# Experts in groups of one larger and two smaller, between pairs, and the first loads rearranged

## The chip, the cores and the metric

The kernel runs on one core of one Trainium2 chip. The time is that of one execution on the device in microseconds. Three runs of the kernel before took 752.1 to 754.06 us, with a median of 753.59 us.

## The reference

One transformer layer on 512 tokens of width 1024, all in fp32: an RMS norm, one input projection that feeds two kinds of attention, one output projection into the residual stream, and then a mixture of 32 SwiGLU experts, of which each token uses two:

```python
h = rms_norm(x, g_attn[l])
proj = h @ w_in[l]                                   # 1024 x 3072
o_da = diff_attention(...)                           # 4 heads, two softmax maps per head
o_sb = stick_breaking(...)                           # 8 heads
x = x + jnp.concatenate([o_da, o_sb], axis=-1) @ w_o[l]
h2 = rms_norm(x, g_ffn[l])
# hier_moe: top-1 of 4 expert groups, then top-2 of 8 experts inside it
y = (jax.nn.silu(xb @ w1[e]) * (xb @ w3[e])) @ w2[e] # 1024 -> 512 -> 1024, for each expert e
```

Each expert has three matrices of 1024x512 fp32, 2 MiB each. All 32 experts are read: 192 MiB, most of the 228.86 MB that the page counts.

## The kernel before, in words

**First part.** The residual input arrives as x transposed (`xT`, eight slices of 128 rows) and as x (`x_t`, four tiles). The input projection's weights come in chunks of 256 columns, each in four pieces of 256 KB (`load_w`). fp32 products are made of rounded parts: ScalarE writes the rounded "high" part (`x_high` for x, `high` in `split_pieces` for weights), VectorE the rest (`x_low`, `low`), and TensorE multiplies the parts (`rows_bundles`, `cols_bundles`). While the first data is on its way, `keep_clock` gives TensorE 20 products of ones. `square` on ScalarE sums the squares of each of the four x tiles, from which `token_scales` makes the norm's factors. `Weave` mixes steps of the projection with the attention tasks; each engine then runs its own instructions in the written order.

**Experts.** Tokens are gathered for a group of experts at a time, 128 rows in all. Each expert has a *place*. The first `FIXED` = 4 places belong to experts 0 to 3, whose weights can be fetched before the routing is known. The rest are sorted by the number of their tokens (`sort_experts`, `name_experts`), so the transfers of a later place need a register that SyncE loads (`values_load` of `who_i`). Places below `SMALL` = 20 have 64 rows (`SLOTS`), the 12 others 32. There are 13 groups: ten pairs of 64-row experts, and at positions 2, 7 and 12 (from 0) a group of four 32-row experts. `hidden` multiplies a group's tokens by w1 and w3 in 16 steps, `outputs` by w2 in 8. A step has one product for each expert of the group; their results lie in different rows of the same PSUM bank. Between the steps stand pieces of the next group's gathering (`quarter`, L1164) and of the last one's return to the tokens (`combine`, L1325 and L1326).

**Transfers.** Every weight part of an expert (half of w1, w3 or w2) is one transfer of 1 MiB by SyncE's queue, into the next tile of a ring (`ring_tile`, list `slots`). The ring goes once through 19 tiles. The two parts of tile `ma` then leave it (`ma` becomes the running sum), so later rounds have 17. A part that has no free tile waits on SyncE until the products that read the tile's last content are done. Group 0's last part goes to `yh` and `yl` (`load_last`). `load_parts(i)` issues group i's transfers: part by part, in each part expert by expert. At group `PAUSE` = 7 stands the `If` of `overflow`, for experts with more tokens than rows.

Of the kernel before, what the change touches and what calls it, by code (L numbers as in the profile page):

```python
# [30 lines left out]
FIXED = 4  # L31
# [63 lines left out]
def tile_block(ctx: ExitStack, tc: tile.TileContext, a: dict, out: bass.AP):  # L95
# [45 lines left out]
    oh_rel, vneg = r_tile[0:32, 0, 0:640], r_tile[0:4, 1, 0:640]  # L141
    lamv, lam_p = r_tile[:, 0, 640:896].rearrange("p (a b) -> p a b", a=4), r_tile[:, 0, 896:960]
    rb = r_tile[0:32, 1, 640:644]
# [44 lines left out]
    g_col = const.tile([P, KC], F32, name="g_col")  # L188
    nc.scalar.dma_start(g_col, a["g_attn"][0].rearrange("(p k) -> p k", k=KC))
# [8 lines left out]
    gqk = const.tile([P, 2], F32, name="gqk")  # L198
    gsub = const.tile([P, 1], F32, name="gsub")
    gsb = const.tile([P, 1], F32, name="gsb")  # L200
    col = lambda ap, n: bass.AP(tensor=ap.tensor, offset=ap.offset, ap=[[1, n], [1, 1]])
    for m in range(2):
        rows = slice(64 * m, 64 * m + 64)
        nc.sync.dma_start(gqk[rows, 0:1], col(a["qn_g"], 64))
        nc.sync.dma_start(gqk[rows, 1:2], col(a["kn_g"], 64))
# [46 lines left out]
    for n in range(KC // 2):  # L252
        x_high(2 * n)
        high[n]()
        x_low(2 * n)
        low[n]()
        x_high(2 * n + 1)
        x_low(2 * n + 1)

    bt = pool_q8.tile([P, 4, 512], F32, tag="bt", name="bt")  # L260
    vdram = dram.tile([4, 640], F32, name="vdram")
    def small_loads():
        nc.sync.dma_start(rb, a["rel_bias"])
        nc.sync.dma_start(oh_rel, a["rel_onehot"])
        for m in range(2):
            nc.sync.dma_start(gsb[64 * m:64 * m + 64], col(a["sb_out_g"], 64))
        nc.sync.dma_start(gsub, col(a["subln_g"], 128))
        for i, n in enumerate(("lam_q1", "lam_k1", "lam_q2", "lam_k2")):
            s = a[n]
            nc.sync.dma_start(lamv[:, i], bass.AP(tensor=s.tensor, offset=s.offset, ap=[[0, P], [1, 64]]))  # L270
# [103 lines left out]
    def h_rows(i):  # L374


        pbs = [bank("mm", (P, 2, 256)) for _ in range(2 if i == 0 else 0)]
        for k in range(0, KC // 2, 2):
            for t0, pb in zip((0, 2), pbs):
                yield from rows_bundles(h_high, h_low, split[i], t0, pb, range(k, k + 2), k == 0, False)  # L380
        for t0 in (0, 2):
            pb = pbs[t0 // 2] if pbs else bank("sc" if (i, t0) == (1, 0) else "mm", (P, 2, 256))
            yield from rows_bundles(h_high, h_low, split[i], t0, pb, range(KC // 2 if pbs else 0, KC), not pbs)
            yield t0, pb
# [261 lines left out]
    for i, (g, n, j) in enumerate(ORDER):  # L646
# [10 lines left out]
    groups = [(0, 2), (2, 2), (20, 4), (4, 2), (6, 2), (8, 2), (10, 2), (24, 4), (12, 2), (14, 2), (16, 2), (18, 2),  # L657
              (28, 4)]
# [3 lines left out]
    slots = [("q8", tag, 2) for tag in ("bt", "qs", "kl", "kh")] + [("xs", "e0", 1), ("xs", "e1", 1)]  # L662
    slots += [("q8", tag, 2) for tag in ("qs", "kl", "kh")] + [("n", "n0", 1), ("n", "n1", 1)]
    slots += [("mx", "ma", 1), ("mx", "ma", 1), ("mx", "mb", 2)]
    slots += [("w8", tag, 2) for tag in ("w_h", "w_l", "w_h", "w_l")]
    slots += [("mx", "mb", 2)]
    slots[0] = ("q8", "bt", 1)

    def ring_tile():

        pool, tag, bufs = slots[ring[0] % len(slots)]
        ring[0] += 1
        if tag == "ma":
            if ring[0] > len(slots):
                return ring_tile()
# [15 lines left out]
    def load_parts(i):  # L691
        last = i == NG - 1
        first, n_exp = groups[i]
        if first < FIXED:
            who = [first + e for e in range(n_exp)]
        else:
            who = [nc.values_load(place_id[0][0:1, first + e:first + e + 1], engines=[mybir.EngineType.SP],
                                  min_val=0, max_val=NE - 1) for e in range(n_exp)]
        t = {}
        for n, h in hidden_order(i) + [("w2", 0), ("w2", 1)]:  # L700
            src = {"w1": w1, "w3": w3, "w2": w2}[n]
# [3 lines left out]
            for c, m in zip(cuts, cuts[1:]):  # L705
                for e in range(n_exp):
                    if (i, n, h, e) == (0, "w2", 1, 1):
                        continue
                    if c == 0:
                        t[n, h, e] = ring_tile()  # L710
                    dst, part = t[n, h, e], expert(who[e], h)(src)
                    if first >= FIXED:
                        part = part.rearrange("o p f -> p (o f)")
                    nc.sync.dma_start(dst[:, c:m], part[:, c:m])
                    if m == 2048:
                        yield t
# [9 lines left out]
    loads, ahead = load_parts(0), load_parts(1)  # L726

# [29 lines left out]
    gfp = const.tile([P, 2, 4], F32, name="gfp")  # L757
# [7 lines left out]
    def router_loads():  # L765
        nc.sync.dma_start(gfp, a["g_ffn"])
        raw_r = pool_at.tile([P, KC, 64], F32, tag="qn", name="raw_r", bufs=2)
        parts = {"w_router_g": raw_r[:, 0:1, 0:32], "w_router_e": raw_r[:, 1:5]}
        for n, r in (("w_router_g", 4), ("w_router_e", 32)):
            parts[n] = parts[n].rearrange("p a b -> p (a b)").rearrange("p (h c) -> p h c", h=2)  # L770
            nc.sync.dma_start(parts[n], a[n].rearrange("p h r c -> p h (r c)"))
        for src, c0, n in ((a["b_router_g"], 0, 4), (a["b_router_e"], 4, 32)):
            nc.sync.dma_start(rbias[:, c0:c0 + n], bass.AP(tensor=src.tensor, offset=src.offset, ap=[[0, P], [1, n]]))
# [14 lines left out]
        def gains():  # L788
            for n, c0, w in (("w_router_g", 0, 4), ("w_router_e", 4, 32)):
                nc.vector.tensor_tensor(wr[:, :, c0:c0 + w], parts[n].rearrange("p h (r c) -> p (h r) c", r=4),  # L790
                                        gfp.rearrange("p h r -> p (h r)").unsqueeze(2).to_broadcast([P, KC, w]),
                                        op=ALU.mult)
# [121 lines left out]
    def match(oh, rk, ts_):  # L914
        n = ts_.stop - ts_.start
        m, w = oh.shape[2:]
# [3 lines left out]
    def gather_part(px, oh, h, ts_):  # L920

        for t in ts_:
            x2 = x_tile[0][:, t, h * 512:(h + 1) * 512].rearrange("p (r b) -> p r b", r=4)
            one = oh[:, t].rearrange("p e s -> p (e s)").bitcast(F32)
# [38 lines left out]
    for t in range(NT):  # L963
        square(t)
    token_scales()
    wv.fill(16)
# [23 lines left out]
    next(ahead)  # L990
# [21 lines left out]
    oh0 = pools["n"].tile([P, NT, 2, SLOTS], F32R, tag="oh", name="oh", bufs=1)  # L1012
    def half_match(n, t):
        for _ in range(n):
            yield
        place(t)
        match(oh0, rank[:, :, 0:2], slice(t, t + 2))
# [32 lines left out]
    for _ in range(7):  # L1050
# [73 lines left out]
    def one_hot(rk, second=False):  # L1124
        n = rk.shape[-1]
        shape = [P, NT, n, P // n]
        if second:
            oh = wk("oht", shape, F32R, bufs=2)
        else:
            oh = pools["n"].tile(shape, F32R, tag="oh", name="oh", bufs=1)  # L1130
        match(oh, rk, slice(0, NT))
        return oh

    def dispatch(oh, p, px=None):
# [3 lines left out]
        ohs = [oh[:, t].rearrange("p e s -> p (e s)") for t in range(NT)]  # L1138
        n_exp, w_exp = oh.shape[2:]
        rows = [slice(w_exp * e, w_exp * e + w_exp) for e in range(n_exp)]  # L1140
        d = {"px": px, "parts": rows}

        spare = not isinstance(p, int)
# [43 lines left out]
        def finish(tag="mm"):  # L1187
# [15 lines left out]
            m = 3 * n_exp  # L1203
            g4 = pools["n"].tile([P, NT, 12], F32, tag="g4" + own, name="g4", bufs=bufs)
            c = 0 if spare else 6 * p
            for u, pb in enumerate(pbs):
                nc.scalar.copy(oht[:, 2 * u:2 * u + 2], pb[:, :, 0])
                nc.vector.tensor_copy(g4[:, 2 * u:2 * u + 2, :m], pb[:, :, 1, c:c + m])
            for e, part in enumerate(rows):
                x = 6 * (e // 2) + 2 * (e % 2)  # L1210
# [118 lines left out]
    def overflow():  # L1329
# [12 lines left out]
        with tc.If(rounds > 0):  # L1342
            move(rank_s[:, :, SMALL:], SLOTS // 2)
            with tc.For_i(0, rounds, 1):
                move(rank_s, -SLOTS)
                with tc.For_i(0, NP, 1) as iv:
# [5 lines left out]
                    dd = dispatch(one_hot(rk), own)  # L1352
# [29 lines left out]
    def group_dispatch(i, oh=None, px=None):  # L1382
        first, n = groups[i]
        if oh is None:
            oh = one_hot((rank if first < FIXED else rank_s)[:, :, first:first + n], i == 1)
        return dispatch(oh, first // 2, px)
# [18 lines left out]
    for i in range(NG):  # L1405
# [3 lines left out]
        if not last:  # L1409
            rest = ahead if i == 0 else load_parts(i + 1)  # L1410
            for nxt in islice(rest, 1) if i == PAUSE else rest:
                pass
        during, after = [[] for _ in range(16)], [[] for _ in range(8)]
        if i == 0:
# [4 lines left out]
            during[1] = [name_experts]  # L1419
# [4 lines left out]
        else:  # L1424
            for n in range(8):
                at_ = (3 if n < 4 else 7) if last else 3 + n // 2 if i == PAUSE else 4 + n // 2 * 2
# [119 lines left out]
```

## Time and profile before

| | |
|---|---|
| median of 3 runs | 753.59 us |
| the profiled execution | 753.97 us, of which the span from first to last instruction is 752.3 us |
| TensorE busy | 726.8 us (97% of the span) |
| VectorE, ScalarE, GpSimd busy | 389.1, 302.2, 91.7 us |
| moved by DMA | 228.86 MB, mean 304 GB/s |
| granted TensorE clock | 0.992 of full speed |

A slice of the page's second part is 18.8 us. Its lines PE and DMA are read together: PE is at 9 tenths nearly throughout, and DMA reaches 9 from the middle on. A busy PE is not one at its best rate, since the records of pipelined products overlap and their ends are modelled; whether TensorE waits is read from the distance between starts.

### The profile page before, as it was taken

The numbers are of one execution on the slowest core, as the hardware profiler recorded it, in microseconds if no ns is written. First come the engines' busy times: TensorE is split into PE (matmuls) and PEld (weight loads), VectorE is DVE, ScalarE is ACT, GpSimd is POOL, SyncE is SP. The second block draws the span as 40 slices with busy tenths as digits, with TensorE's granted clock in tenths as the row PEclk, the third lists the DMA queues.
The fourth block names the chain that finished last, engine by engine and source line by source line (L and its number), as shares of the span: only waits on it lengthen the run. The fifth ranks groups of instructions, "written<-read, shape, count | busy, mean of one in ns | idle before, by whom it ended". The sixth has DMA issues, their size and how long they took to land. (4 is left out here: it accounts for less than half of the span.)

```text
span 752.3 us, 13147 instructions
## 1 busy us (share of the span) xinstructions
PE 726.8 (97%) x4812; PEld 454.7 (60%) x4812; DVE 389.1 (52%) x919; ACT 302.2 (40%) x708; POOL 91.7 (12%) x175
## 2 busy tenths in 40 slices
PE   9999999999999999999999999999779999999986
PEld 9899988887989984554435444453233444535324
DVE  4577778776665462254444554443433544444413
ACT  6665776876755340232232323221222232232100
POOL 0302100466665020000000000000000000000000
PEclk9999999999999999999999999999998999999999
DMA  8432121322573986649999999999999999999998
GB/s 314 134 127 86 54 84 57 113 58 64 166 313 112 368 362 253 240 194 381 418 419 421 421 420 422 421 421 421 416 421 419 423 419 421 422 419 420 418 409 298
DMA packets 46638, 228.86 MB, mean 304 GB/s; under 512 B 6724, under 2 KB 9412, under 8 KB 23656
## 3 DMA queue, kind: packets, MB, share of 16 engines
q1 hardware_dynamic: 46152, 227.83, 76.3%
q8 instruction: 40, 0.66, 0.3%
q14 instruction: 30, 0.25, 0.1%
q10 hardware_dynamic: 416, 0.14, 0.1%
HBM read 225.83 MB, written 2.11 MB: 303 GB/s over the span
## 5 line engine op out<-in xcount | busy, mean ns | idle before, releaser
L1156 ACT CAST part<-xs 128x256 fp32r<-128x256 f32 x176 | 63.1, 406 | 146.6 <-PE ps_mm L1164 60.1
L1157 DVE TENSOR_TENSOR part<-xs,part 128x256 fp32r<-128x256 f32 x176 | 66.6, 419 | 58.7 <-ACT part L1156 58.7
L1327 DVE TENSOR_TENSOR sums<-ps_o,sums 128x512 f32<-128x512 f32 x88 | 56.7, 686 | 71.0 <-PE ps_o L1326 71.0
L313 PE MATMUL ps_mm<-w_h,hTl 128*128 128x256 f32 x240 | 69.3, 289 | 0.1
L1222 PE MATMUL ps_mm<-qs,xt 128*64 128x512 f32 (+1 forms) x136 | 67.8, 610 | 0.0
L313 PE MATMUL ps_mm<-w_h,hTh 128*128 128x256 f32 x240 | 67.3, 281 | 0.0
L313 PE MATMUL ps_mm<-w_l,hTh 128*128 128x256 f32 x240 | 67.3, 280 | 0.0
L1222 PE MATMUL ps_mm<-mb,xt 128*64 128x512 f32 (+1 forms) x120 | 59.0, 610 | 4.1 <-PEq L1342 4.1
L1222 PE MATMUL ps_mm<-kl,xt 128*64 128x512 f32 (+1 forms) x120 | 59.3, 610 | 0.0
L1222 PE MATMUL ps_mm<-w_l,xt 128*64 128x512 f32 (+1 forms) x128 | 50.7, 602 | 0.0
L1222 PE MATMUL ps_mm<-kh,xt 128*64 128x512 f32 (+1 forms) x104 | 50.4, 600 | 0.0
L1222 PE MATMUL ps_mm<-w_h,xt 128*64 128x512 f32 (+1 forms) x120 | 46.8, 601 | 0.0
L313 PEld LDWEIGHTS ps_mm<-w_h,hTl 128*128 128x128 f32 x240 | 45.3, 189 | 0.6 <-DVE qn L438 0.3
L313 PEld LDWEIGHTS ps_mm<-w_l,hTh 128*128 128x128 f32 x240 | 45.3, 189 | 0.1
L313 PEld LDWEIGHTS ps_mm<-w_h,hTh 128*128 128x128 f32 x240 | 45.2, 188 | 0.0
L180 DVE TENSOR_TENSOR w_l<-w_raw,w_h 128x512 fp32r<-128x512 f32 x64 | 44.2, 707 | 1.0 <-ACT w_h L177 0.6
L1325 PE MATMUL ps_o<-yl,oht 128*128 128x512 f32 x96 | 43.2, 450 | 0.6 <-DVE sums L1327 0.6
L518 DVE TENSOR_TENSOR_SCAN p<-p,ones_f 128x513 f32<-128x513 f32 (+3 forms) x32 | 27.5, 858 | 30.5 <-POOL p L513 30.5
L1325 PEld LDWEIGHTS ps_o<-yl,oht 128*128 128x128 f32 x96 | 17.9, 187 | 41.8 <-issue 18.8
L1164 PEld LDWEIGHTS ps_mm<-part,oh 128*128 128x128 f32 x160 | 21.8, 191 | 33.3 <-DVE part L1157 20.3
L1251 DVE SCALAR_TENSOR_TENSOR sl<-ps_mm,rsl,sl 128x256 f32<-128x256 f32 x26 | 11.4, 479 | 58.6 <-PE ps_mm L1222 58.4
L1271 ACT ACTIVATE yh<-ps_sc,gsl 128x512 fp32r<-128x512 f32 (+2 forms) x29 | 18.5, 643 | 55.2 <-PE ps_sc L1278 55.2
(295 smaller groups left out, 1786.5 us busy)
## 6 DMA issues: line engine op xcount, KB each, us to landing
qs<-in_w SPq DMA_DIRECT2D x22, 1024.0 KB, 19.7
e<-in_w SPq DMA_DIRECT2D x22, 1024.0 KB, 19.8
kl<-in_w SPq DMA_DIRECT2D x21, 1024.0 KB, 19.7
kh<-in_w SPq DMA_DIRECT2D x21, 1024.0 KB, 19.7
n<-in_w SPq DMA_DIRECT2D x20, 1024.0 KB, 19.8
mb<-in_w SPq DMA_DIRECT2D x20, 1024.0 KB, 19.8
w_h<-in_w SPq DMA_DIRECT2D x20, 1024.0 KB, 19.8
w_l<-in_w SPq DMA_DIRECT2D x20, 1024.0 KB, 19.7
```

What stands on the lines that cost most here:

```text
L180: eng.tensor_tensor(part(wl, n), raw[i, n], part(wh, n).bitcast(F32), op=ALU.subtract)
L313: nc.tensor.matmul(pb[:, u], lhsT=x(t0 + u, k), rhs=y[:, k], start=first, stop=last, skip_group_check=True)
L518: nc.vector.tensor_tensor_scan(rev, rev, ones_f[:, 0:1].to_broadcast([P, n + 1]), 1.0, op0=ALU.mult, op1=ALU.mult)
L1156: nc.scalar.copy(hi, whole)
L1157: nc.vector.tensor_tensor(lo, whole, hi.bitcast(F32), op=ALU.subtract)
L1164: nc.tensor.matmul(d["rows"][:, q * 256:q * 256 + 256], lhsT=ohs[t], rhs=d[n][:, m], start=(n % 8 == 0 and m == 1), stop=(n % 8 == 7 and m ...
L1222: nc.tensor.matmul(ph[n][part], lhsT=d["xt"][h][:, r, part], rhs=w, start=(h == 0 and r == 0), stop=(h == 1 and r == 3))
L1251: nc.vector.scalar_tensor_tensor(s, ph["w3"][:, c], d["rsl"], s, op0=ALU.mult, op1=ALU.mult)
L1271: nc.scalar.activation(yh, py, AF.Copy, scale=gsl)
L1325: nc.tensor.matmul(pc, lhsT=oht[:, t], rhs=yl[:, c], start=True, stop=False)
L1327: nc.vector.tensor_tensor(sums[0][:, t, cs], pc, (xs if first else sums[0])[:, t, cs], op=ALU.add)
```

## The change

- **Groups.** `FIXED` becomes 3. There are still 13 groups: seven pairs of 64-row experts, and six groups of one 64-row and two 32-row experts, at positions 1, 3, 5, 7, 9 and 12.
- **Order of the transfers.** Group 1 holds expert 2, which is fixed, and two experts whose names come from the routing. Its six fixed parts are issued ahead (into `ma`, `ma`, `w_h`, `w_l`, `w_h`, `w_l`), the twelve others after `name_experts`. The list `slots` is written so that later rounds reuse tiles in the order in which group 1 gives them back.
- **Small parameters.** Gains, the relative bias with its one-hot table, the lambda vectors and the router weights and biases are laid side by side in five arrays. SyncE issues 2 such transfers in place of 13 in the first part, and 2 in place of 5 before the router; ScalarE's one carries more.
- **First chunk.** `keep_clock` has 15 products in place of 20. A one-element copy on ScalarE (`set_up`) stands ahead of the first rounding. Pieces of weights are issued ahead of slices of `xT`, two of the four x tiles behind the second chunk's first pieces, and two of the four squares behind the second chunk's rounding.

```diff
-FIXED = 4
+FIXED = 3
...
+    cols = const.tile([P, 20], F32, name="cols")
+    g_col, gqk, gsub, gsb = cols[:, 0:8], cols[:, 8:10], cols[:, 10:11], cols[:, 11:12]
+    nc.scalar.dma_start(cols, a["cols"])
     load_xT(0, 1)
     load_w()
     load_xT(1, 2)
     for k in range(2, KC, 2):
+        load_w()
         load_xT(k, k + 2)
-        load_w()
-    for t in range(NT):
...
+    load_x(0), load_x(1)
...
+    nc.scalar.copy(const.tile([P, 1], F32, name="set_up"), ones_f[:, 0:1])
...
-    keep_clock(20)
+    keep_clock(15)
...
     for n in range(KC // 2):
+        if n:
+            high[n](), low[n]()
         x_high(2 * n)
-        high[n]()
+        if n == 0:
+            high[n]()
...
+        if n in (1, 2):
+            load_x(n + 1)
...
-    groups = [(0, 2), (2, 2), (20, 4), (4, 2), (6, 2), (8, 2), (10, 2), (24, 4), (12, 2), (14, 2), (16, 2), (18, 2),
-              (28, 4)]
+    pair = lambda p: [(p, SLOTS), (p + 1, SLOTS)]
+    three = lambda p, q: [(p, SLOTS), (q, SLOTS // 2), (q + 1, SLOTS // 2)]
+    groups = [pair(0), three(2, 20), pair(4), three(3, 22), pair(6), three(16, 24), pair(8), three(17, 26), pair(10),
+              three(18, 28), pair(12), pair(14), three(19, 30)]
...
+    slots = early + [ma, ma, w_h, w_l, w_h, w_l, mb, mb] + early[:10]
...
+        for e in fixed:
+            for n, h in order:
+                load(n, h, e, 0, 2048)
+                yield t
...
-    for t in range(NT):
-        square(t)
+    square(0), square(1)
+    wv.fill(8)
+    square(2), square(3)
+    wv.fill(1)
     token_scales()
-    wv.fill(16)
+    wv.fill(7)
...
-            during[1] = [name_experts]
+            during[1] = [name_experts, lambda: list(ahead)]
```

On ScalarE, at the start of the program, these rows stand before (L177 rounds a piece of weights, L236 a slice of xT, L243 is a square):

```order
L236 ACTIVATE hTh<-kh,g_col 128x512
L243 ACTIVATE qs,ss_150<-qs 128x1024 x4
L177 CAST w_h<-w_raw 128x512 x4
L428 ACTIVATE qn<-ps_mm 128x512 x2
L177 CAST w_h<-w_raw 128x512 x2
```

and these now (L176, L235 and L242 are the same three lines):

```order
L235 ACTIVATE hTh<-kh,cols 128x512 x2
L242 ACTIVATE qs,ss_138<-qs 128x1024 x2
L176 CAST w_h<-w_raw 128x512 x4
L242 ACTIVATE qs,ss_138<-qs 128x1024 x2
L427 ACTIVATE qn<-ps_mm 128x512 x2
```

The four roundings of the second chunk stand behind two squares in place of four.

On SyncE, from the end of group 0's transfers on (all `in_w` rows of 128x2048 are parts of experts, `yh` and `yl` are group 0's last part), before:

```order
L714 DMA ma<-in_w 128x2048 x2
L714 DMA mb<-in_w 128x2048
L714 DMA w_h<-in_w 128x2048
L714 DMA w_l<-in_w 128x2048
L714 DMA w_h<-in_w 128x2048
L714 DMA w_l<-in_w 128x2048
L714 DMA mb<-in_w 128x2048
L723 DMA yh<-in_w 128x1024
L723 DMA yl<-in_w 128x1024
L714 DMA bt<-in_w 128x2048
L714 DMA qs<-in_w 128x2048
```

and now (`who_i` holds the names of the sorted experts):

```order
L709 DMA ma<-in_w 128x2048 x2
L709 DMA w_h<-in_w 128x2048
L709 DMA w_l<-in_w 128x2048
L709 DMA w_h<-in_w 128x2048
L709 DMA w_l<-in_w 128x2048
L738 DMA yh<-in_w 128x1024
L738 DMA yl<-in_w 128x1024
L719 TENSOR_LOAD who_i
L719 ISA x2
L719 TENSOR_LOAD who_i
L719 ISA x2
L709 ISA
```

Eight parts of group 1 stand ahead of the names before, six now; everything behind them waits for the names.

On TensorE, the first steps of group 1's hidden products (L1222 before, L1239 now), before:

```order
L1222 MATMUL ps_mm<-ma,xt 64x512 x2
L1164 MATMUL ps_mm<-part,oh 128x256 x4
L1222 MATMUL ps_mm<-ma,xt 64x512 x4
L1164 MATMUL ps_mm<-part,oh 128x256 x4
L1222 MATMUL ps_mm<-ma,xt 64x512 x2
```

and now:

```order
L1239 MATMUL ps_mm<-ma,xt 64x512
L1239 MATMUL ps_mm<-mb,xt 32x512 x2
L1182 MATMUL ps_mm<-part,oh 128x256 x4
L1239 MATMUL ps_mm<-ma,xt 64x512
L1239 MATMUL ps_mm<-mb,xt 32x512 x2
L1239 MATMUL ps_mm<-ma,xt 64x512
L1239 MATMUL ps_mm<-mb,xt 32x512 x2
```

A step was two products of 64 rows; in a group of three it is one of 64 and two of 32.

## Rows read from the trace of the kernel before

**Rows 1.** Windows: us, busy us (count) of PE, PEld, DVE, ACT, POOL, PEclk, DMA share, GB/s

```profile
290.00:300.00 10.00, 9.42 (x57) 5.30 (x58) 1.89 (x5) 0.33 (x1) 0.00 (x0) 1.00 0.86 333
300.00:310.00 10.00, 10.00 (x59) 5.53 (x56) 0.81 (x5) 2.77 (x5) 0.00 (x0) 1.00 0.57 213
310.00:320.00 10.00, 10.00 (x61) 5.55 (x62) 5.04 (x16) 2.51 (x8) 0.00 (x0) 1.00 0.73 254
320.00:330.00 10.00, 10.00 (x52) 4.91 (x48) 4.42 (x10) 3.99 (x10) 0.00 (x0) 1.00 0.67 273
330.00:340.00 10.00, 10.00 (x48) 5.09 (x48) 5.04 (x11) 2.86 (x8) 0.00 (x0) 1.00 0.39 145
340.00:350.00 10.00, 10.00 (x54) 4.45 (x55) 4.85 (x16) 2.39 (x7) 0.00 (x0) 1.00 0.86 339
350.00:360.00 10.00, 10.00 (x64) 3.78 (x64) 4.82 (x11) 3.90 (x10) 0.00 (x0) 1.00 1.00 419
...
650.00:700.00 50.00, 49.99 (x244) 22.67 (x244) 23.05 (x59) 13.80 (x36) 0.00 (x0) 1.00 1.01 421
```

**Rows 2.** The chain that ended last, two of its last pieces: start, us, what

```profile
729.55 10.29 DMA qs<-in_w
...
739.88 1.91 PE ps_sc L1278 x26
```

**Rows 3.** Timeline of SyncE's queue, issues: start, us, engine, line, operation, tiles, count

```profile
255.45 0.91 SPq L714 DMA_DIRECT2D ma<-in_w  x2
...
286.39 0.33 SPq L714 DMA_DIRECT2D bt<-in_w  x1
...
318.05 4.84 SPq L714 DMA_DIRECT2D n<-in_w  x2
335.01 0.33 SPq L714 DMA_DIRECT2D mb<-in_w  x1
...
341.95 0.33 SPq L714 DMA_DIRECT2D w_l<-in_w  x1
```

**Rows 4.** Timeline of PE, first transpose of the hidden values in groups 1, 2, 3

```profile
346.02 0.39 PE L1261 MATMUL ps_mm<-ident,sl 128*128 128x128 f32 x2
...
379.20 0.44 PE L1261 MATMUL ps_mm<-ident,sl 128*128 128x128 f32 x2
...
412.42 0.40 PE L1261 MATMUL ps_mm<-ident,sl 128*128 128x128 f32 x2
```

**Rows 5.** Timeline, outputs to hidden products: pair to pair, then pair to four

```profile
454.46 0.14 PEld L1222 LDWEIGHTS ps_mm<-qs,xt 128*64 128x64 f32 x1 [0.29 <-issue]
454.46 0.59 PE L1278 MATMUL ps_sc<-bt,sl 128*64 128x512 f32 x1
...
454.89 0.59 PE L1222 MATMUL ps_mm<-qs,xt 128*64 128x512 f32 x1
...
518.99 0.59 PE L1278 MATMUL ps_sc<-kl,sl 128*64 128x512 f32 x1
519.51 0.11 PEld L1222 LDWEIGHTS ps_mm<-kh,xt 128*32 128x32 f32 x1 [0.81 <-issue]
519.51 0.62 PE L1222 MATMUL ps_mm<-kh,xt 128*32 128x512 f32 x1
```

**Rows 6.** Timeline of the start: PE, ACT

```profile
1.29 7.46 PE L220 MATMUL ps_mm<-ones_f 128*128 128x128 f32 x40 [1.29 <-DVE ones_f L210]
...
4.25 1.28 ACT L236 ACT_TABLE_LOAD   x1 [4.25 <-DMA kh<-in_xT]
...
8.51 0.36 PE L313 MATMUL ps_mm<-w_h,hTl 128*128 128x256 f32 x1
...
19.54 1.06 ACT L243 ACTIVATE qs<-qs 128x1024 f32<-128x1024 f32 x1 [1.78 <-DMA qs<-in_x]
...
20.60 2.18 ACT L177 CAST w_h<-w_raw 128x512 fp32r<-128x512 f32 x4
...
21.25 0.39 PE L313 MATMUL ps_sc<-w_h,hTl 128*128 128x256 f32 x1 [1.10 <-ACT w_h L177]
```

More of the change, by code (lines that the diff above doesn't have):

```diff
@@ L2 @@
 from functools import partial
-from itertools import islice
 import numpy as np
@@ L193, in tile_block, with load_x @@
     for k in range(2, KC, 2):
+        load_w()
         load_xT(k, k + 2)
-        load_w()
-    for t in range(NT):
+    def load_x(t):
         nc.sync.dma_start(x_t[t], x_in[t])
[L198 to L205, printed above, removed]
+    load_x(0), load_x(1)
     ident = const.tile([P, P], F32, name="ident")
@@ L262, in small_loads @@
     def small_loads():
[L263 to L270, printed above, removed]
+        nc.sync.dma_start(rel, a["rel"])
+        nc.sync.dma_start(lamv, bass.AP(tensor=a["lam"].tensor, offset=a["lam"].offset, ap=[[0, P], [64, 4], [1, 64]]))
     def bias_rows():
@@ L377, in h_rows @@
         pbs = [bank("mm", (P, 2, 256)) for _ in range(2 if i == 0 else 0)]
-        for k in range(0, KC // 2, 2):
+        for k in range(0, KF, 2):
             for t0, pb in zip((0, 2), pbs):
@@ L382, in h_rows @@
             pb = pbs[t0 // 2] if pbs else bank("sc" if (i, t0) == (1, 0) else "mm", (P, 2, 256))
-            yield from rows_bundles(h_high, h_low, split[i], t0, pb, range(KC // 2 if pbs else 0, KC), not pbs)
+            yield from rows_bundles(h_high, h_low, split[i], t0, pb, range(KF if pbs else 0, KC), not pbs)
             yield t0, pb
@@ L692, in load_parts, with load @@
         last = i == NG - 1
[L693 to L701, printed above, removed]
+        who, t = {}, {}
+        def load(n, h, e, c, m):
+            place = groups[i][e][0]
+            if place >= FIXED and e not in who:
+                who[e] = nc.values_load(place_id[0][0:1, place:place + 1], engines=[mybir.EngineType.SP], min_val=0,
+                                        max_val=NE - 1)
+            if c == 0:
+                t[n, h, e] = ring_tile()
+            part = expert(who.get(e, place), h)({"w1": w1, "w3": w3, "w2": w2}[n])
+            if place >= FIXED:
+                part = part.rearrange("o p f -> p (o f)")
+            nc.sync.dma_start(t[n, h, e][:, c:m], part[:, c:m])
+        order = hidden_order(i) + [("w2", 0), ("w2", 1)]
+        fixed = [e for e, (place, _) in enumerate(groups[i]) if place < FIXED] if i == 1 else []
+        for e in fixed:
+            for n, h in order:
+                load(n, h, e, 0, 2048)
+                yield t
+        for e in range(len(groups[i])) if i == 1 else ():
+            if e not in fixed:
+                who[e] = nc.values_load(place_id[0][0:1, groups[i][e][0]:groups[i][e][0] + 1],
+                                        engines=[mybir.EngineType.SP], min_val=0, max_val=NE - 1)
+        for n, h in order:
             cuts = (0, 1024, 2048) if last and n + str(h) in ("w31", "w20") else (0, 2048)
@@ L705, in load_parts @@
             for c, m in zip(cuts, cuts[1:]):
-                for e in range(n_exp):
-                    if (i, n, h, e) == (0, "w2", 1, 1):
+                for e in range(len(groups[i])):
+                    if (i, n, h, e) == (0, "w2", 1, 1) or e in fixed:
                         continue
[L709 to L714, printed above, removed]
+                    load(n, h, e, c, m)
                     if m == 2048:
@@ L726, in tile_block @@
     loads, ahead = load_parts(0), load_parts(1)
+    second = []
     x_tile = []
@@ L765, in router_loads @@
     def router_loads():
[L766 to L773, printed above, removed]
+        raw_r = pool_at.tile([P, KC, 64], F32, tag="qn", name="raw_r", bufs=2).rearrange("p k c -> p (k c)")
+        raw_r = raw_r[:, :KC * 36].rearrange("p (k c) -> p k c", c=36)
+        nc.sync.dma_start(raw_r, a["w_router"])
+        src = a["b_router"]
+        nc.sync.dma_start(rbias, bass.AP(tensor=src.tensor, offset=src.offset, ap=[[0, P], [1, 36]]))
         nc.gpsimd.iota(desc, pattern=[[-1, 4]], base=4, channel_multiplier=0, allow_small_or_imprecise_dtypes=True)
@@ L788, in gains @@
         def gains():
[L789 to L792, printed above, removed]
+            nc.vector.tensor_tensor(wr, raw_r, cols[:, 12:20].unsqueeze(2).to_broadcast([P, KC, 36]), op=ALU.mult)
         wv.chain((12, gains))
@@ L989, in tile_block @@
         wv.step()
-    next(ahead)
+    second.append(next(ahead))
     wv.fill(3)
@@ L1049, in tile_block @@
     gather_part(px, oh0, 1, (2,))
-    for _ in range(7):
+    for _ in range(5):
         next(ahead)
@@ L1122, in wk, with one_hot @@
         return work.tile(list(shape), dt, tag=tag, name=tag, bufs=bufs)
-    def one_hot(rk, second=False):
-        n = rk.shape[-1]
-        shape = [P, NT, n, P // n]
+    def one_hot(parts, second=False):
         if second:
-            oh = wk("oht", shape, F32R, bufs=2)
+            oh = wk("oht", [P, NT, P], F32R, bufs=2)
         else:
-            oh = pools["n"].tile(shape, F32R, tag="oh", name="oh", bufs=1)
-        match(oh, rk, slice(0, NT))
+            oh = pools["n"].tile([P, NT, P], F32R, tag="oh", name="oh", bufs=1)
+        c = 0
+        for rk, w in parts:
+            n = rk.shape[-1] * w
+            match(oh[:, :, c:c + n], rk, slice(0, NT), w)
+            c += n
         return oh
     def dispatch(oh, p, px=None):
-        ohs = [oh[:, t].rearrange("p e s -> p (e s)") for t in range(NT)]
-        n_exp, w_exp = oh.shape[2:]
-        rows = [slice(w_exp * e, w_exp * e + w_exp) for e in range(n_exp)]
+        ohs = [oh[:, t] for t in range(NT)]
+        spare = not isinstance(p, list)
+        places = [(e, SLOTS) for e in range(2)] if spare else p
+        rows, c = [], 0
+        for _, w in places:
+            rows.append(slice(c, c + w))
+            c += w
+        twos = sorted({e // 2 for e, _ in places})
         d = {"px": px, "parts": rows}
-        spare = not isinstance(p, int)
         def gather(h, ts_=tuple(reversed(range(NT)))):
@@ L1382, in group_dispatch @@
     def group_dispatch(i, oh=None, px=None):
[L1383 removed]
+        g = groups[i]
         if oh is None:
[L1385 to L1386 removed]
+            cuts = [(g[0][0], 2, SLOTS)] if len(g) == 2 else [(g[0][0], 1, SLOTS), (g[1][0], 2, SLOTS // 2)]
+            oh = one_hot([(rank_s[:, :, c:c + n], w) for c, n, w in cuts], i == 1)
+        return dispatch(oh, g, px)
     d = group_dispatch(0, oh0, px)
@@ L1410, in tile_block @@
             rest = ahead if i == 0 else load_parts(i + 1)
-            for nxt in islice(rest, 1) if i == PAUSE else rest:
+            nxt = second[0] if i == 0 else next(rest)
+            for _ in () if i in (0, PAUSE) else rest:
                 pass
```

70 lines of the change are left out of this document (37 added, 33 removed).

## The prediction

> **What bounds the kernel now.** I read the page's slices first, then the chain that ended last, then windows around the place where the bound changes, then SyncE's queue there, then TensorE's steps in that place.
>
> The slices show two halves. In the first, TensorE is at 9 tenths or more while DMA is far from full. In the second both are at 9. The windows tell which of the two ends last there: from 350 us on the DMA share is 1.00 and stays there, at 419 to 421 GB/s [rows 1]. The chain agrees: its last transfer takes 10.29 us from 729.55 and lands near 739.84, and the last products follow it [rows 2]. So from 350 us to 740 us the end is set by how many bytes are still to come, and behind them stand 752.3 - 739.84 = 12.46 us of last products, sums and stores.
>
> Between 290 and 350 us it is otherwise. The six windows have 333, 213, 254, 273, 145 and 339 GB/s [rows 1], 15.57 MB in 60 us, where 421 GB/s would give 25.26 MB. The missing 9.69 MB are 23.0 us of an idle queue, 11.0 us before 320 and 12.0 us after. TensorE is full there: the transfers wait for tiles that TensorE has not yet given back. SyncE issues two parts from 318.05 (the second one 4.5 us later), and then nothing until 335.01 [rows 3]. The reason is in the ring: the first four products of group 1 read the tiles `ma`, filled from 255.45 on [rows 3], and these are not reused, so what group 1 finishes first opens no slot.
>
> Before 290 us the transfers of experts wait for routing or tiles, and TensorE's own work sets the pace.
>
> A group takes TensorE 33.2 us, whether it has four experts or two: the first transposes of groups 1, 2 and 3 start at 346.02, 379.20 and 412.42, and group 2 is one of four [rows 4]. The queue needs 1,048,576 B / 421 GB/s = 2.49 us a part, so 29.9 us for a pair, 44.8 us for three experts and 59.8 us for four. TensorE's total, 13 x 33.2 = 432 us, is below the queue's 192 x 2.49 = 478 us.
>
> **The change part by part.**
>
> *The start.* TensorE begins its first real product at 8.51 us, directly behind 40 records of the 20 products of ones, which cover 7.46 us [rows 6]. Ten records fewer are at most 10 x 7.46 / 40 = 1.9 us; the last of them run at the higher clock and are shorter than the mean, so I take 1.1 us. The operands allow that: the table load of 1.28 us at 4.25 [rows 6] now stands ahead of the wait for xT, and the first rounded parts follow that much earlier. Next, TensorE waits 1.10 us at 21.25 for the second chunk's rounding, which stands behind the fourth square, and that square waits 1.78 us for its tile of x [rows 6]. Now two squares stand behind the rounding, two tiles of x behind the second chunk's first pieces, and four tiny transfers are gone from SyncE's queue ahead of these pieces. The wait goes; next late are the pieces themselves, behind 3 MB of xT and weights and 1 MB of x, which at 2.49 us a MiB are there some 10 us after the queue starts, ahead of TensorE's need at about 20 us. I take 1.1 + 1.1, and 0.3 us for a second wait behind it: 2.5 us, with bounds of 0 (the pieces are late after all, or later waits in the attention part absorb it) and 1.9 + 1.5 = 3.4 us. TensorE's chain runs on from there to the first expert, so all of it arrives there.
>
> *The other small loads* are off the path of TensorE, beside projection and attention. I take 0, between -0.5 and +0.5 us.
>
> *The transfers around the routing.* Six parts of group 1 are loaded ahead in place of eight, so 2 x 2.49 = 5.0 us of transfers move behind the names. Their two tiles (`mb`) are free by then, and a free queue takes them: before, the first part behind the routing was issued at 286.39 [rows 3], and the names come at about that place. They fill 5.0 of the 11.0 us that were idle before 320 us. SyncE waits for the names with everything queued behind, but there are only two free tiles to be filled in that time, and group 1 starts some 35 us later.
>
> *Group 1.* Its quarters of hidden products and its two output halves now give back 2, 2, 3, 3, 3 and 3 tiles, where they gave 0, 2, 2, 2, 2 and 2. The first two come when the first four steps are done, near 329 us, not at 335.01; the next at about 335; and with the three of the third quarter, near 342 (before, SyncE issued `w_l` there at 341.95 [rows 3]), the queue has more than it can move. Of the 12.0 us idle after 320 I count 7 as filled (the two parts of 329, 5.0 us, and some 2 us of the time between 340 and 350). Together 5.0 + 7.0 = 12.0 us less idle, of which 5.0 pay for the two parts moved back: 7.0 us gained. A second count, by parts that land: 13 behind the routing by 328, six more by about 349 against 15 in the same time before, so four more, less the two moved back, is two parts or 5.0 us. I take 6 us; bounds are 0 (the names come late enough to cost what the tiles give) and 12 us (every idle us after 320 filled).
>
> *The later groups.* The bytes are the same, and the queue ought to stay full: a pair and a three need 74.7 us of transfers and 66.4 us of TensorE. So the order of groups in itself gives nothing more at the end, as long as a three takes TensorE no longer than a pair. That is the open point. No row shows products of 64 and of 32 rows beside each other. The nearest rows are a change from pair to four. Between equal shapes the next weights load 0.43 us ahead, at 454.46, while the last outputs run, and the products start 0.43 us after those of the step before, at 454.89. From 64 to 32 rows the weights load only at 519.51, and the products start 519.51 - 518.99 = 0.52 us after the last: 0.09 us more, and nothing loaded ahead [rows 5]. But there every row of the array was in use by the step before, so it doesn't show whether a product of 32 rows waits for one of 64 in *other* rows. Price per step from below: 0. From above: the products of 64 and the two of 32 take turns, each 0.43 us with 0.09 us for each change, 1.04 us in place of 0.43. With 24 steps, 0 to 14.6 us for a three. I take 0, since four products on separate rows already take no longer than two (the 33.2 us of [rows 4]), and the array may well keep its books by rows and not by shape.
>
> The Trainium skill speaks against this. "TensorEngine Tiling (Array Packing)", section "Tiling Modes", says that a change of the tiling mode, and not just of the tile, drains the engine. The trace agrees that a change costs something (the 0.09 us and the late weights of [rows 5]); by the rule each step of a three would change modes twice, and the sum would be that of the first rival below.
>
> *Sum.* 753.97 (the profiled execution, 0.38 above the median) - 2.5 - 6.0 = 745.5 us; less 0.4 for the median, **745 us**.
>
> **The rivals.**
>
> *Shapes take turns.* A three costs TensorE 33.2 + 14.6 = 47.8 us, more than its 44.8 us of transfers. Then TensorE is the bound: from 282.4 - 2.5 = 279.9, seven pairs and six threes are 232 + 287 = 519 us, so products end near 799, and with the stores the time is about 803 us. It decides from about 0.25 us a step on: TensorE's slack over all groups is 478 - 432 = 46 us, less some 10 us of last products behind the last landing, over 6 x 24 = 144 steps. For it: the weights that are not loaded ahead at a change of shape. Against it: those rows show no free part of the array.
>
> *A change costs, but shapes run together.* At 0.09 us twice a step, 4.3 us a three, 26 us in all. It stays within that slack, but the last group, whose outputs follow the last bytes, and the first, whose tiles open the queue, are later by 4 us: about 749 us.
>
> *The queue is filled, the start isn't.* If the start's 2.5 us are lost in waits of the attention part, 747.5 us; if also the names come late and only 2 us of the queue's idle time are won, 751.6 us.
>
> *The whole idle time goes.* If the queue is full from 320 us on and the start gives 3.4 us, 753.6 - 12 - 3.4 = 738 us.
>
> **How the numbers follow.** 0.3% is 2.3 us, about what a measurement of this kernel can tell from no change. The forecast has 0.52, the second rival 0.14, the third 0.10, the fourth 0.06, the turns 0.16, and 0.02 is left for other losses. Faster by more than 0.3% (below 751.3 us) are the forecast, the second and fourth, and most of the third: 0.79. Within 0.3%: 0.04. Slower: 0.17. The range is 738 to 755 us: it takes in all but the turns, which lie apart near 803 us; no width short of 65 us would take them in.
>
> **What would show it.** In the profile after, the first projection product starts near 7.4 us, without the wait of 1.10 us at 21; the windows from 320 us on (2.5 us earlier) have more than 400 GB/s from 340 on, and the gap in SyncE's issues at 323 to 335 is cut in two; the last landing is near 731 us; and in group 1 the products of 64 and 32 rows of one step start within 0.05 us of each other, with steps 0.43 us apart. If instead the two shapes start 0.5 us apart, steps are 1.04 us apart, DMA drops below 1.00 in the second half and the chain runs through TensorE, then the first rival holds and the forecast is wrong.

## The result, and the profile after

The changed kernel takes 885.85 us (median of 4 runs, 884.2 to 886.29), the kernel before 753.83 us beside it (4 runs, 752.1 to 754.24). The ratio is 1.1756, 95% interval 1.1737 to 1.1775. The forecast of 745 us was wrong, and so was its sign. What came is the rival that had 0.16, "shapes take turns", and even this rival, with 803 us, had less than half of the loss.

The page after is read in the same order as that of before: slices first, then the chain.

```profile
PE   9999999999999999999999999999999999999998
...
DMA  8332213138294865799788988898789978999603
...
PE 29%; DVE 0%; issue 0%; ACT 0%; DVEq 0%
PE ps_mm L1239 14%; PE ps_sc L1295 8%; PE ps_o L1342 1%; PE ps_sc L1182 1%; PE ps_mm L1182 1%; PE ps_o L1343 1%; PE ps_tr L1194 1%; PE ps_mm L1278 0%; PE ps_mm L1495 0%; PE ps_o L1212 0%; PE ps_o L1495 0%; DVE sums L1344 0%; PE ps_sc L219 0%; ACT st L1188 0%; DVE sl L1268 0%
...
qs<-in_w SPq DMA_DIRECT2D x22, 1024.0 KB, 6.8
```

The last of these rows reads in the page of before

```profile
qs<-in_w SPq DMA_DIRECT2D x22, 1024.0 KB, 19.7
```

DMA is at 7 to 9 tenths in most of the second half where it was at 9, no transfer is left among the chain's engines, and a part of 1 MiB lands 6.8 us after its issue (the median of 22), against 19.7 us before: the queue no longer has a backlog. TensorE is the bound. L1239 (hidden products, L1222 before) and L1295 (outputs, L1278 before) lead the chain.

The same chain, in order of time (start, us, what), has a three from 723.30 and a pair from 770.54:

```profile
723.30 9.93 PE ps_mm L1239 x30
...
770.54 4.44 PE ps_mm L1239 x20
```

The profile has two records for each fp32 product of these steps: the 20 products of ones leave 40 in [rows 6]. A step of a pair is four records, a step of a three six. So 30 records are five steps of a three, 9.93 / 5 = 1.99 us each, and 20 records are five steps of a pair, 4.44 / 5 = 0.89 us each. TensorE's timeline at the first steps of group 1 (start, us, engine, line, operation, tiles, shape, count) shows why:

```profile
325.34 1.07 PE L1239 MATMUL ps_mm<-ma,xt 128*64 128x512 f32 x2
326.34 1.05 PE L1239 MATMUL ps_mm<-mb,xt 128*32 128x512 f32 x4
327.33 1.07 PE L1239 MATMUL ps_mm<-ma,xt 128*64 128x512 f32 x2
```

The two products of 32 rows start 1.00 us after that of 64 rows and not beside it, and the next product of 64 rows waits 0.99 us for them: a step is 327.33 - 325.34 = 1.99 us. The loads of the array tell the same (the same columns; what is loaded are a product's tokens, and the expert's weights stream past them):

```profile
322.74 0.14 PEld L1239 LDWEIGHTS ps_mm<-ma,xt 128*64 128x64 f32 x1 [0.28 <-issue]
323.69 0.14 PEld L1239 LDWEIGHTS ps_mm<-mb,xt 128*32 128x32 f32 x4 [0.81 <-issue]
```

As in [rows 5], the load for the new shape starts only when the old shape is through.

The first transposes of the hidden values (L1278, L1261 in [rows 4]) stand at

```profile
313.32 0.38 PE L1278 MATMUL ps_mm<-ident,sl 128*128 128x128 f32 x2
...
365.15 0.41 PE L1278 MATMUL ps_mm<-ident,sl 128*128 128x128 f32 x2 [0.59 <-DVE sl L1268]
...
406.93 0.39 PE L1278 MATMUL ps_mm<-ident,sl 128*128 128x128 f32 x2
...
456.94 0.39 PE L1278 MATMUL ps_mm<-ident,sl 128*128 128x128 f32 x2
...
854.56 0.80 PE L1278 MATMUL ps_mm<-ident,sl 128*128 128x128 f32 x4 [0.75 <-DVE sl L1268]
```

From group 1 (a three) to group 2 (a pair) it is 41.78 us, and from group 2 to group 3 (a three) 50.01 us, where [rows 4] have 33.2 us for each. The first of these distances holds the outputs of a three (8.6 us more), the second the hidden half of the next three (16.8 us more): 25.4 us for a three. The twelve distances from 313.32 to 854.56 are 541.2 us; six of 50.0, five of 41.8 and one of 33.2 make 542.2. Six threes cost TensorE 6 x 25.4 = 152 us, and the kernel is 132.0 us slower; the rest, by the runs below, had been time in which TensorE could wait for the queue.

The windows (columns as in [rows 1]):

```profile
290.00:300.00 10.00, 9.36 (x50) 5.22 (x46) 1.19 (x4) 0.34 (x1) 0.00 (x0) 0.83 1.01 422
...
330.00:340.00 10.00, 10.00 (x38) 2.99 (x38) 1.95 (x6) 2.47 (x7) 0.00 (x0) 1.00 0.55 210
...
650.00:700.00 50.00, 50.00 (x219) 19.26 (x220) 20.02 (x49) 13.56 (x34) 0.00 (x0) 1.00 0.92 367
```

The first has 422 GB/s where it had 333: the two parts moved behind the names fill the queue there. From 330 on (and much the same to 350) the slow group 1 gives tiles back late, and at 650 the queue has 367 GB/s, not 421. TensorE's PE column is 10.00 of 10 from 300 us on; that it spends this time on turns is to be read only from starts and steps.

### The profile page after: what moved, and what is told of

Its sections match the earlier page's. It is cut to its first block, busy times and chain, and to the rows that moved or that the text cites. A ratio compares the mean times of both kernels' runs of the same rounds, so it can differ in the third digit from the quotient of the medians.

```text
span 884.7 us, 13076 instructions
## 1 busy us (share of the span) xinstructions
PE 870.2 (98%) x4778; PEld 466.9 (53%) x4778; DVE 391.4 (44%) x936; ACT 302.3 (34%) x709; POOL 92.2 (10%) x175
## 5 line engine op out<-in xcount | busy, mean ns | idle before, releaser
L1239 PE MATMUL ps_mm<-kl,xt 128*64 128x512 f32 (+1 forms) x128 | 65.6, 607 | 0.0
L1239 PE MATMUL ps_mm<-w_l,xt 128*64 128x512 f32 (+1 forms) x112 | 57.8, 608 | 0.0
L1239 PE MATMUL ps_mm<-qs,xt 128*64 128x512 f32 (+1 forms) x112 | 57.5, 607 | 0.0
L1239 PE MATMUL ps_mm<-kh,xt 128*64 128x512 f32 (+1 forms) x112 | 56.2, 604 | 0.0
L1239 PE MATMUL ps_mm<-w_h,xt 128*64 128x512 f32 (+1 forms) x104 | 53.5, 607 | 0.0
L1239 PE MATMUL ps_mm<-mb,xt 128*64 128x512 f32 (+1 forms) x144 | 51.9, 605 | 0.0
L1289 DVE SCALAR_TENSOR_TENSOR yl<-ps_sc,gsl,yh 128x512 fp32r<-128x512 f32 (+2 forms) x29 | 20.1, 695 | 67.0 <-ACT yh L1288 63.5
L1239 PE MATMUL ps_mm<-n,xt 128*64 128x512 f32 (+1 forms) x104 | 48.7, 607 | 0.0
L1282 ACT COPY sl<-ps_mm 128x256 f32<-128x256 f32 x26 | 10.0, 386 | 102.3 <-PE ps_mm L1278 102.3
```

The lines of the kernel that those rows point to most:

```text
L1239: nc.tensor.matmul(ph[n][part], lhsT=d["xt"][h][:, r, part], rhs=w, start=(h == 0 and r == 0), stop=(h == 1 and r == 3))
L1289: nc.vector.scalar_tensor_tensor(yl, py, gsl, yh.bitcast(F32), op0=ALU.mult, op1=ALU.subtract)
```

## The experiments

Four theories were put to the chip: the turns, as the profile after shows them; the order of the groups and the transfers as such; the rearranged start; and, beside the turns, the question how much of them is the change of shape and how much the missing overlap.

### One shape in a three

Kernel: the changed one, but in a group of three the 64-row expert's product is given as two of 32 rows, with the same weights streamed twice. Bytes, groups, names and tiles are those of the changed kernel.

```diff
+        d["units"] = list(enumerate(rows))
+        if len(rows) == 3:
+            d["units"] = [(0, slice(0, 32)), (0, slice(32, 64)), (1, rows[1]), (2, rows[2])]
...
-                for e in range(len(d["parts"])):
-                    hidden_product(ph, d, n, h, r, e, t[n, h, e][:, r * HID:(r + 1) * HID])
+                for e, part in d["units"]:
+                    hidden_product(ph, d, n, h, r, part, t[n, h, e][:, r * HID:(r + 1) * HID])
...
-                for e, part in enumerate(d["parts"]):
+                for e, part in d["units"]:
```

> The changed kernel, with the 64-row expert of a group of three computed as two products of 32 rows each on the same weights, so that a step has four products of one shape. Theory (products of 64 and of 32 rows take turns on the array, and a step of a three costs 1.99 us in place of 0.86): a three takes the 33.1 us of a pair again, the queue is the bound from about 340 us on, and the time is 753.6 less 1.3 (TensorE reaches the first expert at 281.1 in place of 282.4) less about 6 of idle queue: 746 us, between 740 and 752. Rival (the threes are slow for another reason: their transfers come late, or the ring of tiles blocks them): steps stay near 2 us and the time above 850 us.

Measured: 747.4 us (6 runs, 746.33 to 750.0), ratio to the kernel before 0.9923 (0.9904 to 0.9943). The turns explain the whole loss: with one more product in each step of a three the kernel is 138 us faster, and 5.5 us faster than the kernel before beside it (752.87 us, 17 runs). TensorE's timeline in group 1:

```profile
322.65 0.62 PE L1241 MATMUL ps_mm<-ma,xt 128*32 128x512 f32 x2
322.67 0.62 PE L1241 MATMUL ps_mm<-mb,xt 128*32 128x512 f32 x2
323.11 0.60 PE L1241 MATMUL ps_mm<-ma,xt 128*32 128x512 f32 x2
...
323.54 0.60 PE L1241 MATMUL ps_mm<-ma,xt 128*32 128x512 f32 x2
```

All four products of a step start within 0.02 us of each other, their second records follow 0.46 us later and the next step 0.43 us behind these, so a step is 323.54 - 322.65 = 0.89 us. The transposes of groups 1, 2 and 3 are 33.2 us apart again:

```profile
347.08 0.41 PE L1280 MATMUL ps_mm<-ident,sl 128*128 128x128 f32 x2 [0.59 <-DVE sl L1270]
...
380.26 0.39 PE L1280 MATMUL ps_mm<-ident,sl 128*128 128x128 f32 x2
...
413.37 0.43 PE L1280 MATMUL ps_mm<-ident,sl 128*128 128x128 f32 x2
```

With the turns gone, this run also shows what the rest of the change does. First its windows, then SyncE's issues, then its chain:

```profile
290.00:300.00 10.00, 9.36 (x58) 5.40 (x55) 1.19 (x4) 0.34 (x1) 0.00 (x0) 1.00 1.01 424
300.00:310.00 10.00, 10.00 (x60) 5.58 (x59) 0.82 (x5) 2.77 (x5) 0.00 (x0) 1.00 0.69 265
310.00:320.00 10.00, 10.00 (x62) 5.59 (x60) 5.31 (x19) 2.66 (x9) 0.00 (x0) 1.00 0.83 312
320.00:330.00 10.00, 10.00 (x78) 3.91 (x78) 4.36 (x10) 4.45 (x11) 0.00 (x0) 1.00 0.80 304
330.00:340.00 10.00, 10.00 (x71) 3.96 (x69) 4.28 (x8) 2.85 (x7) 0.00 (x0) 1.00 0.90 341
340.00:350.00 10.00, 9.40 (x68) 3.77 (x68) 5.18 (x14) 1.80 (x6) 0.00 (x0) 1.00 0.98 395
...
720.00:735.00 15.00, 13.02 (x126) 5.81 (x128) 3.05 (x6) 1.70 (x4) 0.00 (x0) 1.00 0.95 370
```

```profile
316.58 4.84 SPq L709 DMA_DIRECT2D n<-in_w  x2
326.28 0.92 SPq L709 DMA_DIRECT2D mb<-in_w  x2
331.77 0.33 SPq L709 DMA_DIRECT2D bt<-in_w  x1
```

```profile
723.95 10.01 DMA w_l<-in_w
734.00 1.91 PE ps_sc L1297 x26
```

The six windows from 290 to 350 add up to 20.41 MB, against 15.57 MB in [rows 1]: 4.84 MB more, 11.5 us at 421 GB/s. 5.0 us of that pay for the two parts moved behind the names, so 6.5 us are gained. SyncE's gap behind the issue of `n` ends at 326.28, where in [rows 3] it ended at 335.01. The last part lands at 723.95 + 10.01 = 733.96, 5.9 us ahead of the 739.84 of [rows 2].

The change also holds something that its list doesn't name: in group 1 the eight pieces of group 0's return to the tokens (`combine`) stand at steps 8 to 15 of the hidden products, where they stood at 4 to 10. The second quarter of group 1 is free of them, and its tiles come back at 331.77 (`bt`), where the prediction had 335. How much of the 6.5 us this gives, no run shows.

### The rearranged start alone

Kernel: the one before, with only the small parameters side by side and the first chunk's loads, roundings and squares as changed; groups and transfers as before.

```diff
-    keep_clock(20)
+    keep_clock(15)
...
-    for t in range(NT):
-        square(t)
+    square(0), square(1)
+    wv.fill(8)
+    square(2), square(3)
+    wv.fill(1)
...
```

> The kernel before with only the small parameters laid side by side and the first chunk's loads, roundings and squares rearranged; groups as before. By the trace of the changed kernel, whose first expert begins 1.3 us earlier: 752.5 us. By the term of the prediction (2.5 us): 751.3. If the rearranged start is lost behind the idle queue before 340 us: 753.8.

Measured: 753.4 us (12 runs, 752.71 to 754.4), ratio 1.0005 (0.9995 to 1.0016). The start gives nothing that can be measured at the end. In this run the first expert's products start at 281.58, against 282.36 before, and the last part lands at

```profile
728.76 10.06 DMA qs<-in_w
```

738.82, 1.0 us earlier than in [rows 2], in single profiled executions.

### The old start with the new groups

Kernel: "one shape in a three", with the start and the small loads of the kernel before. The diff is that of the run above, turned round.

> Groups of three in one shape, as in one_shape, but with the small parameters and the first chunk as in the kernel before. If the 1.3 to 1.5 us by which one_shape reaches its first expert earlier arrive at the end: 747.4 + 1.4 = 748.8 us. If they are lost, as front_only alone makes one expect (753.4 against 752.87): 747 us, no difference from one_shape.

> The same kernel as one_shape, timed again beside old_start on one chip, so that the two can be compared: 747 us, 0.992 of the kernel before.

Measured on one chip: 747.05 us with the old start (6 runs, 746.5 to 749.89; ratio 0.9919, 0.99 to 0.9938) and 748.08 us with the new one (6 runs, 746.11 to 749.4; ratio 0.9925, 0.9907 to 0.9943). The intervals lie upon each other: with these groups too the start is worth nothing that can be measured. Its first expert starts at

```profile
280.58 0.64 PE L1246 MATMUL ps_mm<-bt,xt 128*64 128x512 f32 x1 [0.52 <-DVE xt L1210]
```

which is 1.78 us ahead of the kernel before with the same start. Most of that is there by 20 us. ScalarE's fourth square, which in [rows 6] waits 1.78 us for its tile of x and starts at 19.54, stands in this run at

```profile
18.14 1.06 ACT L242 ACTIVATE qs<-qs 128x1024 f32<-128x1024 f32 x1 [0.97 <-DMA qs<-in_x]
```

and the second chunk's first product follows at 19.86 in place of 21.25, 1.39 us earlier, though the two programs issue the same up to there. So the waits that the prediction read in [rows 6] differ by more than a microsecond between two executions of the same start, and the first expert's earlier start in the changed kernel can't be put down to the rearranged loads.

### Products of a three ordered by shape within a quarter

Kernel: the changed one; within each quarter of a three (four steps) the four products of the 64-row expert come first, then the eight of the others. The outputs are ordered in the same way, but for those of the last group. The work is the same, the number of changes smaller.

```diff
+            three = len(d["parts"]) == 3
+            for r in range(4 if three else 0):
+                hidden_product(ph, d, n, h, r, 0, t[n, h, 0][:, r * HID:(r + 1) * HID])
             for r in range(4):
-                for e in range(len(d["parts"])):
+                for e in range(1 if three else 0, len(d["parts"])):
...
```

> The changed kernel, with the products of a three ordered by shape inside each quarter: four of 64 rows, then four steps of two of 32 rows. Two changes of shape in a quarter in place of eight, apart from the other work between steps. Theory (turns: each shape has its 0.86 us, and a change 0.13 us): 6 changes x 0.13 x 6 quarters = 4.8 us a three, 28 us in all: about 857 us. Rival (the products could overlap, and each change itself costs (1.99 - 0.86) / 2 = 0.57 us): three quarters of the changes gone are about 20 us a three, 100 us or more in all, below 790 us.

Measured: 867.4 us (one run), 18.5 us below the changed kernel. The timeline of its group 1:

```profile
320.71 3.60 PE L1239 MATMUL ps_mm<-ma,xt 128*64 128x512 f32 x8
324.24 1.05 PE L1239 MATMUL ps_mm<-mb,xt 128*32 128x512 f32 x4
...
325.89 1.91 PE L1239 MATMUL ps_mm<-mb,xt 128*32 128x512 f32 x8
327.73 0.74 PE L1182 MATMUL ps_mm<-part,oh 128*128 128x256 f32 x4
```

Four 64-row products behind each other take 324.24 - 320.71 = 3.53 us, 0.88 us each, and two steps of 32 rows 327.73 - 325.89 = 1.84 us, 0.92 us each. Each shape alone takes as long as a whole step of one shape; the two together are 0.88 + 0.92, and the 1.99 us of the changed kernel hold some 0.2 us more for two changes. The time says much the same: 18.5 us over the 6 x 6 x 6 = 216 changes that the expectation counts as gone are 0.09 us each, the 0.09 us of [rows 5] and not the 0.13 us of the expectation, which therefore came out 10 us too low. So of the 1.1 us that a step loses, about 0.9 are the missing overlap, which ordering doesn't give back, and only the rest is the change.

### Mixed shapes in the kernel before

Kernel: the one before, but in the pairs at positions 3 to 6 the second expert is given as two products of 32 rows beside the first one's 64. Groups, transfers and bytes are those of before.

```diff
+    def units(d):
+        rows = d["parts"]
+        if d.get("mixed"):
+            return [(0, rows[0]), (1, slice(64, 96)), (1, slice(96, 128))]
+        return list(enumerate(rows))
...
+        d["mixed"] = 3 <= i <= 6
...
```

> The kernel before, with the second expert of the pairs at positions 3 to 6 computed as two products of 32 rows beside the first one's 64. Same groups, transfers and results; only the shapes in a step are mixed. Theory (turns): a step of these four pairs goes from 0.86 to about 1.99 us, a pair from 33.1 to about 59 us, 102 us in all; TensorE's total becomes 534 us behind 282.4, so about 822 us, between 800 and 850. Rival (mixed shapes overlap, and the slowness belongs to groups of three): 753.6 us and steps of 0.86 us.

Measured: 838.49 us (one run). Its timeline and its windows:

```profile
396.85 1.07 PE L1221 MATMUL ps_mm<-mb,xt 128*64 128x512 f32 x2
397.86 1.05 PE L1221 MATMUL ps_mm<-w_h,xt 128*32 128x512 f32 x4
398.84 1.07 PE L1221 MATMUL ps_mm<-w_l,xt 128*64 128x512 f32 x2
```

```profile
500.00:550.00 50.00, 50.00 (x184) 15.37 (x182) 12.98 (x32) 9.37 (x25) 0.00 (x0) 1.00 0.58 217
...
650.00:700.00 50.00, 49.32 (x288) 21.87 (x280) 24.84 (x63) 16.81 (x44) 0.00 (x0) 1.00 1.01 420
```

Steps of 1.99 us again, and 217 GB/s amid these groups against 420 behind them. The transposes of these groups,

```profile
488.89 0.38 PE L1266 MATMUL ps_mm<-ident,sl 128*128 128x128 f32 x2
...
547.58 0.38 PE L1266 MATMUL ps_mm<-ident,sl 128*128 128x128 f32 x2
```

are 58.69 us apart, 25.5 us more than in [rows 4], which is the price of a three in the changed kernel to 0.1 us. The mixing of shapes alone does it, without the new groups and without the new order of the transfers.

### One shape in the outputs only

Kernel: the changed one, with the two products of 32 rows in place of 64 only in the output steps of a three; its hidden steps stay mixed.

> The changed kernel with one shape in the output steps of a three alone; its hidden steps keep products of 64 and 32 rows. Theory (turns, TensorE the bound): the output half of a three falls from 17.3 to 8.7 us, 6 x 8.6 = 52 us in all, 885.9 - 52 = 834 us. Rival (a part of the slowness hangs on the hidden steps alone, or the queue takes over): 860 us or more.

Measured: 831.38 us (one run), 54.5 us below the changed kernel and 84.0 above "one shape in a three". Six output halves were to give 6 x 8.6 = 51.6 us, six hidden halves 6 x 16.8 = 100.8. The price adds up step by step, but the first 17 us of it are not paid: that much TensorE can lose in "one shape in a three" while the queue is the bound.

## Why the prediction was wrong

**The step that failed** is the one of the later groups: "I take 0", for a step with both shapes. Its reason was that "the array may well keep its books by rows and not by shape". It did not in any step that was read: products of 64 and 32 rows took turns in the changed kernel, in "products ordered by shape" and in the mixed pairs, though their rows are disjoint. The row that showed it was there, the late loads in [rows 5], and the argument set it aside since every row of the array had been in use. That was a reason to keep both ends, not to take the lower one: an unknown price between 0 and 14.6 us, of which the kernel had slack for a part only, made the loss at least as likely as the gain; by the prediction's own count the loss began at 0.25 us of a span from 0 to 0.61 us a step. The rule cited then, that a change of the tiling mode drains TensorE (the Trainium skill, "TensorEngine Tiling (Array Packing)", section "Tiling Modes"), agrees with what the runs show; it says nothing of the price, which is 25.4 us a three here.

**The price was mis-sized as well.** The upper bound of 1.04 us a step took one record of 0.43 us for a product. A product has two, as the 40 records of the 20 products of ones in [rows 6] show, so a pair's step is 0.89 us and a mixed one 1.99. 1.1 us more in 24 steps would be 26.4 us; 25.4 were measured, probably since beside 128-wide work a change of shape is due anyway. The rival's 803 us with 6 x (25.4 - 14.6) = 65 us more are 868. Of the 18 us left, 8.5 are in the first group: from its first products at 281.11 to its transposes at 313.32 it takes 32.2 us, where a later pair's hidden half takes 23.7 us (group 2, from 383.23 to 406.93). Another 8.0 us are in the last group, whose outputs come in narrower steps: its last product ends at 880.6, 26.1 us behind its transposes, where the outputs of group 1 take 18.1 us (365.15 to 383.23). And 1.2 us are the first products, at 281.11 and not at 279.9.

**The point from which the rival decides** was too generous. 46 less 10 us of slack gave 0.25 us a step. The runs with mixed shapes leave 152 - 138.5 = 14 us (the changed kernel), 101 - 84 = 17 us (one shape in the outputs only) and 4 x 25.5 - (838.49 - 752.87) = 16 us (mixed pairs) unpaid. The 46 us set all 192 parts of the queue against TensorE's groups, but 19 of them, 47 us of transfers, had been issued before the first expert's products at 282.36, and the 23 us in which the queue stood idle were left out: 478 - 47 + 23 - 432 is 22 us, and less the same 10 us it is 12 us. With 14 to 17 us of slack over 144 steps the kernel gets slower from about 0.1 us a step on. By that the second rival, 26 us with shapes running together, would have been slower too, and not 749 us.

**The transfers around the routing and group 1** were right: 12.0 us less idle, 5.0 to be paid, 6 us gained were predicted; with one shape 11.5 us less idle and 5.9 us at the last landing were measured. The two parts moved behind the names filled the first window as told, and the first two tiles of group 1 came back at 326 us.

**The start** was wrong in its end. The first product starts 1.81 us earlier (1.1 was taken; ten records fewer took off the mean price, not that of the short ones). The wait of 1.10 us at 21.25 is gone, with the second chunk's first product at 19.54. But TensorE now waits 0.73 us at 10.59 for the low part of a slice of xT, and 0.34 us at 22.71: the second chunk's last two pieces are late after all. SyncE issues them only at 11.82 and 13.77, where the prediction had them landed some 10 us after the queue starts (ScalarE's roundings, the same columns as in [rows 6]):

```profile
6.70 0.36 PE L312 MATMUL ps_mm<-w_h,hTl 128*128 128x256 f32 x1
...
19.27 0.62 ACT L176 CAST w_h<-w_raw 128x512 fp32r<-128x512 f32 x1 [1.59 <-DMA w_raw<-in_w_in]
21.31 0.62 ACT L176 CAST w_h<-w_raw 128x512 fp32r<-128x512 f32 x1 [1.42 <-DMA w_raw<-in_w_in]
...
22.71 0.39 PE L312 MATMUL ps_sc<-w_l,hTh 128*128 128x256 f32 x1 [0.34 <-DVE w_l L179]
...
281.11 0.64 PE L1239 MATMUL ps_mm<-bt,xt 128*64 128x512 f32 x1 [0.52 <-DVE xt L1202]
```

At the first expert 1.25 us are left of the 2.5 predicted, and the run with the start alone, at 1.0005, shows that none of it can be measured at the end. That the start's 2.5 us are lost, as in the third rival, is what happened; where they are lost was not shown, and the 1.10 us wait was in part that of one execution ("the old start with the new groups"). With the turns left out, that rival's 747.5 us is what the kernel takes: 747.4 and 748.08.

**Small loads:** 0 was taken, and the two comparisons of the start, which hold them too, show no difference that can be measured.

## What to carry to other kernels

Products of 64 and of 32 rows that shared TensorE's array here ran beside those of their own shape and not beside the other: before mixing experts of two sizes in a step, look at the starts of both shapes, or write the larger as several products of the smaller shape, which cost no time here (33.2 us a group either way). Other shapes were not run. A term that no row of a profile shows, and whose bounds reach across the sign of the whole change, is not to be taken at the end that suits the change; here one run of mixed pairs in the old kernel would have told it. Count the records of a product before its duration is taken from one.

## What the runs showed that was not expected

- Two shapes on disjoint rows take turns in full, 0.88 and 0.92 us with some 0.2 us for two changes, 1.99 us a step, in two kernels with different groups.
- Streaming an expert's weights twice, for two products of 32 rows in place of one of 64, costs nothing beside others of that shape: 33.2 us a group, as for a pair of 64 rows. This version, at 0.9923 and 0.9925 of the kernel before, is the fastest that was run, with either start.
- In the last 15 us up to about 1 us behind the last landing, "one shape in a three" has 370 GB/s (720 to 735), the kernel before 390 (726 to 741). The difference, 0.3 MB or 0.7 us, takes back a part of the 6.5 us won around 320.
- In the changed kernel the granted clock has a mean of 0.83 in 290 to 300, and of 0.50 (1.2 GHz) from 296 to 298, behind a wait of TensorE of 0.64 us that ends at 295.35; from 300 on it is 1.00. The first group takes 32.2 us there, and 30.6 us in "one shape in a three", where the same wait is 0.65 us long and the clock stays at 1.00. It isn't the change that does it: "mixed shapes in the kernel before" has the drop too (0.83 in 290 to 300, a first group of 32.0 us), and up to there its program is that of the kernel before, which shows 1.00. What decides between the two is open.
